# A transformer stack on one core: convolution inputs earlier in the mixing stage, output projection split 7 + 1, activation rows of 2048 bytes

## The chip, the cores and the metric

The kernel runs as one program on one core of a Trainium2 chip. The metric is device microseconds of one execution. All arithmetic is fp32; every dense product is built from three matmuls of a split number format (see below). TensorE (PE) does the matmuls, VectorE (DVE) and ScalarE (ACT) the elementwise work, GpSimd (POOL) a small triangular recurrence, and SyncE (SP) issues most of the DMA transfers.

## The reference, cut to what matters

Three residual blocks follow one another on a sequence of 512 tokens with 1024 channels: a token-mixing block with a first feed-forward network, then an attention block and a gated linear recurrence, each with a feed-forward network, on 528 tokens (16 meta tokens are put in front). The change concerns the first block, above all its token mixing:

```
p = h @ w_in
p_conv, p_rw = p[..., :2 * CONV_WIDTH], p[..., 2 * CONV_WIDTH:]
u, u_gate = jnp.split(p_conv, 2, axis=-1)
u = u * jax.nn.sigmoid(u_gate)
u = causal_dwconv(u, conv_dw_w, conv_dw_b)          # 31 taps, 512 channels
u = jax.nn.silu(layer_norm(u) * conv_ln_g + conv_ln_b)
...
y = wkv7_scan(rh, heads(decay), kh, vh, kk, heads(a))   # 8 heads of 64
...
m = jnp.concatenate([u, y], axis=-1) @ w_out            # 1024 x 1024
x = x + gt_m * rms_norm(m, mix_post_g)
h = rms_norm(x, ffn_pre_g) * (1.0 + sc_f) + sh_f        # input of the first FFN
f = channel_mix(h, w_up, ffn_dw_w, ffn_dw_b, w_down)    # 1024 -> 5632 -> 1024
```

## The kernel before, in words

Channels lie on the 128 partitions and tokens along the free dimension, so an activation of 1024 channels is eight K tiles of 128 x 512. A dense product splits its operands into a high and a low part: activations into xh and xl, weights into wh (a cast on ACT, L167) and wl (a subtraction on DVE, L168). For each K tile three matmuls follow: xh with wh, xh with wl, xl with wh (L192, L193, L194; all are called `mm` after the PSUM tile they write). The PSUM pool of `mm` has two buffers, and each is emptied by ACT or DVE before it is used again.

The two tiles xh and xl hold the input of whichever dense product comes next. Each has eight rows per partition, one per K tile, of 544 floats (2176 bytes), and 512-token stages read from an offset within a row (SEG1). The feed-forward's hidden activations, gh and gl, have rows of 512 floats (2048 bytes).

**The mixing stage** works on four pairs of heads. `wkv_prep` makes the operands of a pair; `wkv_inverse` inverts 128 x 128 triangles in blocks of doubling size (POOL does the smallest blocks, PE matmuls L714 to L751 the others); `wkv_tail` goes through four chunks of the sequence (L766 to L795) and then normalises: a per-token statistic by matmul (L274), a reciprocal square root of eleven small DVE operations on 128 x 8 (L294 to L305), a broadcast back by matmul (L285), the gate (L803, L804) and the product with it (L805). Beside it four convolution tiles are made: `conv_in(i)` is two dense products of 24 matmuls, `conv(i)` the first tap on ACT and 30 taps on DVE (L496, 120 in all). `ada_tile` multiplies 24 weight tiles with the conditioning vector on DVE (L328), as they arrive by DMA.

`mix_out` ends the stage: the output projection, in which the concatenated K tiles are three wkv tiles (pairs 0 to 2), four convolution tiles and the fourth wkv tile. The convolution tiles need the layer norm over all 512 channels (`conv_tail`, L541 to L564), the last wkv tile the tail of pair 3. Before, K tiles 0 to 2 are multiplied first for all eight output tiles (72 matmuls, parked by an ACT copy, L894), and the other five for the first four output tiles at 512 columns and for the last four in two token halves (`dense_ends`; DVE adds L905 and L909). Then RMS norm, residual (`post`, L814 and L815), second RMS norm (L849) and the FFN's input (L926 to L928), each per half.

The order of instructions on an engine is set by a scheduler with priorities: what is written in a `with filler(k)` block takes a very low priority, so it goes where an engine has nothing more urgent, and its place among the rest is not seen in the code.

## Time and profile before

| | |
|---|---|
| median of 3 runs | 2323.74 us (2323.18 to 2327.2) |
| profiled execution | 2322.99 us |
| its span, first to last instruction | 2319.9 us |
| mean granted TensorE clock | 0.987 |
| mixing stage | 0 to 471.6 us of the span |
| first FFN | 471.6 to about 850 us |

The profile gives each engine's busy time, the rows of each instruction with its start within the span, the idle time before it and what ended that idle time. Matmuls overlap in the array: a row's own duration includes the drain, so the price of a matmul in a stream is the distance from its start to the start of the next.

### The profile page before, as it was taken

The page shows a single profiled execution, that of the slowest core. Times are in us where ns is not written, and L with a number is a line of the kernel's source. Part 1 is how long each engine was busy: PE and PEld are TensorE (multiplying, and loading weights), DVE is VectorE, ACT ScalarE, POOL GpSimd, SP SyncE. Part 2 cuts the span into 40 slices and gives each one's busy share as a digit, 9 for nine tenths or more (in the row PEclk, how much of TensorE's full clock was granted, in tenths as well). Part 3 has the DMA queues.
Part 4 walks back from the last instruction along what each step waited for, and adds up shares of the span by engine and source line. Part 5 has one row for each costly group of instructions (what it writes and reads, how often), then busy time and mean ns, then how long its engine had stood idle before and what let it go on. Part 6 is the DMA issues. An engine that isn't in the chain of part 4 may idle for free.

```text
span 2319.9 us, 38166 instructions
## 1 busy us (share of the span) xinstructions
PE 2245.9 (97%) x15368; PEld 1986.3 (86%) x15368; DVE 1428.8 (62%) x3061; ACT 963.0 (42%) x1898; POOL 73.1 (3%) x163
## 2 busy tenths in 40 slices
PE   7989898899999999999999999999999999999999
PEld 4657675678888889988799999999999999999888
DVE  6856777775553376666676666435666667666522
ACT  3533234544442365566654444324333335444311
POOL 1140320000000000000000000000000000000000
PEclk8999999899999999999999999999999999999999
DMA  8443321252223432221032222333121113232232
GB/s 306 140 132 107 97 54 53 86 163 94 97 91 92 128 121 85 71 74 56 31 109 92 91 91 86 92 88 120 56 65 56 53 38 113 91 98 94 89 118 75
DMA packets 97487, 220.10 MB, mean 95 GB/s; under 512 B 21264, under 2 KB 43024, under 8 KB 97312
## 3 DMA queue, kind: packets, MB, share of 16 engines
q1 hardware_dynamic: 94112, 213.84, 29.3%
q10 hardware_dynamic: 2912, 3.69, 0.5%
q8 instruction: 121, 1.98, 0.4%
q0 software_dynamic: 288, 0.15, 0.1%
q14 instruction: 54, 0.44, 0.1%
HBM read 211.24 MB, written 6.85 MB: 94 GB/s over the span
## 4 chain that ended last, share of the span: by engine, by line
PE 85%; DVE 6%; DMA 3%; ACT 2%; POOL 2%; issue 1%; SPq 0%; ACTq 0%; DVEq 0%; POOLq 0%
PE mm L193 23%; PE mm L192 23%; PE mm L194 23%; PE sb L1385 3%; DVE wl L168 1%; PE sc L1200 1%; POOL Tb L698 1%; PE sb L1175 1%; DMA wa<-ada_wT 1%; PE sc L1218 1%; POOL tm L696 1%; ACT wh L167 1%; PE sa L849 1%; PE sa L1105 1%; PE sa L658 0%
## 5 line engine op out<-in xcount | busy, mean ns | idle before, releaser
L192 PE MATMUL mm<-xh,wh 128*128 128x264 f32 (+4 forms) x2852 | 906.2, 318 | 11.2 <-ACT xh L251 5.7
L193 PE MATMUL mm<-xh,wl 128*128 128x264 f32 (+4 forms) x2852 | 898.6, 315 | 2.3 <-DVE wl L168 2.1
L194 PE MATMUL mm<-xl,wh 128*128 128x264 f32 (+4 forms) x2852 | 896.5, 314 | 0.1
L192 PEld LDWEIGHTS mm<-xh,wh 128*128 128x128 f32 x2852 | 535.4, 188 | 48.4 <-ACT xh L251 6.7
L193 PEld LDWEIGHTS mm<-xh,wl 128*128 128x128 f32 x2852 | 537.0, 188 | 39.9 <-DVE wl L168 4.5
L168 DVE TENSOR_TENSOR wl<-ws,wh 128x1024 fp32r<-128x1024 f32 (+3 forms) x358 | 399.4, 1116 | 273.3 <-ACT wh L167 272.3
L194 PEld LDWEIGHTS mm<-xl,wh 128*128 128x128 f32 x2852 | 535.5, 188 | 34.4 <-issue 3.4
L167 ACT CAST wh<-ws 128x1024 fp32r<-128x1024 f32 (+3 forms) x358 | 344.7, 963 | 470.6 <-PE mm L194 402.4
L193 PE MATMUL mm<-gh,wl 128*128 128x264 f32 (+2 forms) x792 | 253.3, 320 | 1.3 <-DVE wl L168 0.9
L192 PE MATMUL mm<-gh,wh 128*128 128x264 f32 (+2 forms) x792 | 253.0, 319 | 0.0
L194 PE MATMUL mm<-gl,wh 128*128 128x264 f32 (+2 forms) x792 | 252.7, 319 | 0.0
L193 PEld LDWEIGHTS mm<-gh,wl 128*128 128x128 f32 x792 | 149.6, 189 | 13.3 <-DVE wl L168 2.8
L192 PEld LDWEIGHTS mm<-gh,wh 128*128 128x128 f32 x792 | 149.5, 189 | 10.4
L194 PEld LDWEIGHTS mm<-gl,wh 128*128 128x128 f32 x792 | 149.6, 189 | 10.3
L959 DVE SCALAR_TENSOR_TENSOR fz<-mm,V,fz 128x511 f32<-128x511 f32 x88 | 65.9, 748 | 69.7 <-ACT fz L957 68.1
L496 DVE SCALAR_TENSOR_TENSOR h<-u,cw,h 128x512 f32<-128x512 f32 x120 | 90.1, 753 | 3.7 <-ACT h L494 2.9
L1385 PE MATMUL sb<-q,kt 128*128 128x64 f32 (+3 forms) x592 | 75.4, 271 | 2.3 <-DVE kt L1417 2.3
L1385 PEld LDWEIGHTS sb<-q,kt 128*128 128x128 f32 x592 | 73.3, 195 | 2.8 <-DVE kt L1417 1.0
L193 PE MATMUL mm<-oh,wl 128*128 128x264 f32 x256 | 75.0, 293 | 0.5 <-DVE wl L168 0.5
L192 PE MATMUL mm<-oh,wh 128*128 128x264 f32 x256 | 74.6, 291 | 0.0
L194 PE MATMUL mm<-ol,wh 128*128 128x264 f32 x256 | 74.4, 291 | 0.0
L957 ACT ACTIVATE fz<-mm,V 128x512 f32<-128x512 f32 x44 | 34.3, 779 | 67.8 <-PE mm L194 67.7
(499 smaller groups left out, 2781.8 us busy)
## 6 DMA issues: line engine op xcount, KB each, us to landing
ws<-w_up_t SPq DMA_DIRECT2D x44, 512.0 KB, 3.7
ws<-gate_t SPq DMA_DIRECT2D x44, 512.0 KB, 3.7
ws<-up_t SPq DMA_DIRECT2D x44, 512.0 KB, 3.6
...
```

The costliest lines, as they stand in the source:

```text
L167: nc.scalar.copy(hi[:, :n], st[:, :n])
L168: nc.vector.tensor_sub(lo[:, :n], st[:, :n], hi[:, :n])
L192: mm(o, hi[:, w], xh[i][:, a:b], start=start and i == 0, stop=False)
L193: mm(o, lo[:, w], xh[i][:, a:b], start=False, stop=False)
L194: mm(o, hi[:, w], xl[i][:, a:b], start=False, stop=stop and i == n - 1)
L496: nc.vector.scalar_tensor_tensor(acc, src, w, acc, MULT, ADD)
L696: nc.gpsimd.tensor_tensor(tm[:, 0:n, 0:w], Gb[:, j, w:].unsqueeze(2).to_broadcast([64, n, w]), Tb[:, j, 0:w].unsqueeze(1).to_broadcast([64 ...
L698: nc.gpsimd.tensor_tensor(o, o, tm[:, 0:n, 0:w], op=ADD)
L849: nc.tensor.matmul(sq.ps[:, :n], k.mean, t, start=i == 0, stop=i == KD - 1)
L957: nc.scalar.activation(z, ps, AF.Identity, bias=vec("ffn_dw_b", nt), scale=wt(2))
L959: nc.vector.scalar_tensor_tensor(z[:, t:], ps[:, 0:T1 - t], wt(2 - t), z[:, t:], MULT, ADD)
L1385: nc.tensor.matmul(o, kt[:, a:a + P], qv, start=True, stop=True)
```

## The change

Three things change, and all of them keep the arithmetic.

First, the rows: within the 512-token stages (mixing and the first FFN) xh and xl are now read through views x1h and x1l, whose rows have 512 floats (2048 bytes). For the later stages the rows become 530 floats (2120 bytes). The two columns of zeros at the head of the later rows are written after the first FFN.

Second, the convolution: `conv_in(1)`, `conv_in(2)` and `conv_in(3)` stand ahead of the tails of pairs 0, 1 and 2, and all taps are fillers.

Third, the output projection: K tiles 0 to 6 of all output tiles first, then K tile 7 for the eight output tiles, all at 512 columns; the squares for the RMS norm are summed by matmul (L853 in the changed kernel, L849 before) instead of by DVE adds, and there is one reciprocal square root over 512 columns where there were two over 256.

```diff
-SEG1 = [(2, 514)]
-SEG1X = [(2, 258), (258, 514)]
+SEG1 = [(0, T1)]
+SEG1X = [(0, H1), (H1, T1)]
...
-    k.xh, k.xl = (k.res.tile([P, KD, T2 + 16], F32R, name=n)[:, :, 6:6 + T2 + 2] for n in ("xh", "xl"))
-    nc.gpsimd.memset(k.xh[:, :, 0:2].bitcast(F32), 0.0)
-    nc.gpsimd.memset(k.xl[:, :, 0:2].bitcast(F32), 0.0)
+    both = [k.res.tile([P, 67 * 64], F32R, name=n) for n in ("xh", "xl")]
+    k.xh, k.xl = (t[:, :KD * (T2 + 2)].rearrange("p (k t) -> p k t", k=KD) for t in both)
+    k.x1h, k.x1l = (t[:, :KD * T1].rearrange("p (k t) -> p k t", k=KD) for t in both)
...
+        def conv_late(i):
+            with filler(k):
+                conv(i)
+
         conv_in(0)
         gates()
-        conv(0)
+        conv_late(0)
         wkv_inverse(k, Q[0])
+        conv_in(1)
         wkv_tail(k, Q[0])
         Q[2] = pair(2)
+        conv_late(1)
         wkv_inverse(k, Q[1])
-        conv_in(1)
+        conv_in(2)
         wkv_tail(k, Q[1])
-        conv(1)
+        conv_late(2)
         Q[3] = pair(3)
-        conv_in(2)
         wkv_inverse(k, Q[2])
-        with filler(k):
-            conv(2)
+        conv_in(3)
+        conv_late(3)
         wkv_tail(k, Q[2])
-        conv_in(3)
         wkv_inverse(k, Q[3])
-        conv(3)
...
+        conv_tail(k, p2, S.acc_u)
         for i in range(KD):
-            if i == 2:
-                conv_tail(k, p2, S.acc_u)
-            dense(k, A["w_out_t"][i], k.xh, k.xl, SEG1, lambda j, ps: nc.scalar.copy(m[i], ps), kts=(3,))
+            dense(k, A["w_out_t"][i], k.x1h, k.x1l, SEG1, lambda j, ps: nc.scalar.copy(m[i], ps), kts=(7,))
...
-    def evac(i, j, ps):
-        if j is None:
-            nc.vector.tensor_add(m[i], m[i], ps)
-            add_square(k, sq, i, 0, m[i], T1)
-            return
-        mt = m[i][:, hs(j)]
-        nc.vector.tensor_add(mt, mt, ps[:, 0:H1])
-        add_square(k, sq, i, H1 * j, mt, H1)
-        if i == KD - 1:
-            rms_scale(k, sq, H1 * j, H1, r[j])
+    def evac(i, ps):
+        nc.vector.tensor_add(m[i], m[i], ps)
+        add_square(k, sq, i, 0, m[i], T1, True)
+
+    for i in range(KD):
+        dense(k, A["w_out_t"][i][:, 7 * P:], k.x1h, k.x1l, SEG1, lambda _, ps: evac(i, ps), kts=(1,), x0=7)
     r = p2.tile([P, T1], F32, name="r", tag="tl", bufs=1)
+    rms_scale(k, sq, 0, T1, r, True)
     r = [r[:, hs(j)] for j in range(2)]
-    w = [A["w_out_t"][i][:, 3 * P:] for i in range(KD)]
-    dense_ends(k, w, k.xh, k.xl, SEG1X, evac, 4, SEG1[0], kts=(5,), x0=3)
...
-        nc.gpsimd.memset(k.rp[:, 0:2], 0.0)
+        for t in (k.rp[:, 0:2], *(t[:, :, 0:2].bitcast(F32) for t in (k.xh, k.xl))):
+            nc.gpsimd.memset(t, 0.0)
```

How the engines' orders move is shown at three places. The line numbers are each kernel's own; in this part of the changed kernel they are one to four higher than before.

PE at the end of the inverse of pair 0 and the start of its tail, before (X, Dt and NM are operands of the recurrence, `mm` the dense products):

```order
L742 MATMUL sb<-Dt,ys 64x64 x4
L751 MATMUL sb<-X,Dt 128x128 x8
L766 MATMUL sa<-NM_106,X 64x128 x2
L771 MATMUL sa<-tok,X 128x128
L766 MATMUL sa<-NM_106,X 64x128 x2
L771 MATMUL sa<-tok,X 128x128
L766 MATMUL sa<-NM_106,X 64x128 x2
```

The same place in the changed kernel, the last seven rows from where the dense run ends:

```order
L755 MATMUL sb<-X,Dt 128x128 x8
L194 MATMUL mm<-xh,wl 128x512
L195 MATMUL mm<-xl,wh 128x512
L193 MATMUL mm<-xh,wh 128x512
...
L193 MATMUL mm<-xh,wh 128x512
L194 MATMUL mm<-xh,wl 128x512
L195 MATMUL mm<-xl,wh 128x512
L770 MATMUL sa<-NM_104,X 64x128 x6
L775 MATMUL sa<-tok,X 128x128 x2
L782 MATMUL sa<-tok 128x128
L783 MATMUL sa<-X,tok 128x128
```

Between the last matmul of the inverse and the first of the tail now stand 26 dense matmuls of 512 columns; before there was none. Between the statistic (L274, now L275) and the broadcast (L285, now L286) of that tail there are 45 of them, before 12.

DVE in the tail of pair 3, from the statistic onward, before (rsxb, tstb and rstb are the small operands of the reciprocal square root, `h<-u,cw,h` is a tap of the convolution, wl a split of weights):

```order
L305 TENSOR_SCALAR rsxb<-sb 128x8
L496 SCALAR_TENSOR_TENSOR h<-u,cw,h 128x512
L294 TENSOR_SCALAR tstb<-rsxb 128x8
L168 TENSOR_TENSOR wl<-ws,wh 128x384
L496 SCALAR_TENSOR_TENSOR h<-u,cw,h 128x512
L295 TENSOR_SCALAR tstb<-tstb 128x8
L496 SCALAR_TENSOR_TENSOR h<-u,cw,h 128x512
L297 TENSOR_TENSOR rstb<-tstb 128x8
L168 TENSOR_TENSOR wl<-ws,wh 128x384
L496 SCALAR_TENSOR_TENSOR h<-u,cw,h 128x512
L298 SCALAR_TENSOR_TENSOR rstb<-rstb,rsxb 128x8
```

The same in the changed kernel:

```order
L306 TENSOR_SCALAR rsxb<-sb 128x8
L295 TENSOR_SCALAR tstb<-rsxb 128x8
L296 TENSOR_SCALAR tstb<-tstb 128x8
L298 TENSOR_TENSOR rstb<-tstb 128x8
L299 SCALAR_TENSOR_TENSOR rstb<-rstb,rsxb 128x8
L300 SCALAR_TENSOR_TENSOR tstb<-rstb,tstb 128x8
L298 TENSOR_TENSOR rstb<-tstb 128x8
```

No tap and no split of weights stands between the small operations any more; all taps lie ahead of this tail. On PE, no dense matmul stands in the tail of pair 3 either, where 54 stood before.

PE at the end of the output projection in the changed kernel, with buffer numbers (mm_3319 is the seven-K-tile part of the last output tile, mm_3447, mm_3462 and mm_3476 the one-K-tile parts of the first three, sa_3460 the sum of squares):

```order
L193 MATMUL mm_3319<-xh_88,wh_3322 128x512
L193 MATMUL mm_3447<-xh_88,wh_3450 128x512
L194 MATMUL mm_3447<-xh_88,wl_3451 128x512
L195 MATMUL mm_3447<-xl_89,wh_3450 128x512
L194 MATMUL mm_3319<-xh_88,wl_3323 128x512
L195 MATMUL mm_3319<-xl_89,wh_3322 128x512
L193 MATMUL mm_3319<-xh_88,wh_3322 128x512
L194 MATMUL mm_3319<-xh_88,wl_3323 128x512
L193 MATMUL mm_3462<-xh_88,wh_3465 128x512
L194 MATMUL mm_3462<-xh_88,wl_3466 128x512
L195 MATMUL mm_3462<-xl_89,wh_3465 128x512
L853 MATMUL sa_3460<-nsq_3458,mean_79 128x512
```

It goes on so, three matmuls and one square at a time, to the eighth one-K-tile part, and only then come the last 13 matmuls of mm_3319. Before, the same engine ran through four groups of 15 matmuls at 512 columns and eight of 15 at 256:

```order
L192 MATMUL mm_3431<-xh_88,wh_3434 128x512
L193 MATMUL mm_3431<-xh_88,wl_3435 128x512
L194 MATMUL mm_3431<-xl_89,wh_3434 128x512
L192 MATMUL mm_3457<-xh_88,wh_3460 128x256
L193 MATMUL mm_3457<-xh_88,wl_3461 128x256
L194 MATMUL mm_3457<-xl_89,wh_3460 128x256
```

## Rows read from the trace of the kernel before

**Rows 1.** The page: busy time, share of the span and instructions of each engine.

```profile
PE 2245.9 (97%) x15368; PEld 1986.3 (86%) x15368; DVE 1428.8 (62%) x3061; ACT 963.0 (42%) x1898; POOL 73.1 (3%) x163
```

**Rows 2.** Stretches: us, busy us (count) of PE, PEld, DVE, ACT, POOL, PEclk, DMA.

```profile
368.60:405.30 36.70, 29.68 (x149) 19.49 (x148) 28.55 (x58) 16.54 (x28) 0.10 (x1) 0.97 0.22 67
405.30:437.20 31.90, 31.66 (x182) 27.77 (x182) 20.90 (x38) 17.93 (x30) 0.00 (x0) 0.92 0.39 116
437.20:460.00 22.80, 12.34 (x39) 8.74 (x40) 22.51 (x57) 12.57 (x32) 0.00 (x0) 0.78 0.04 11
...
471.60:784.00 312.40, 311.37 (x1337) 251.65 (x1338) 171.09 (x213) 122.53 (x159) 0.00 (x0) 1.00 0.35 108
```

**Rows 3.** Timeline of PE, first FFN, up projection (start us, us, what).

```profile
559.71 0.40 PE L192 MATMUL mm<-xh,wh 128*128 128x512 f32 x1
...
561.82 0.39 PE L192 MATMUL mm<-xh,wh 128*128 128x512 f32 x1
```

**Rows 4.** Timeline of PE, first FFN, down projection.

```profile
769.82 0.39 PE L194 MATMUL mm<-gl,wh 128*128 128x512 f32 x1
...
771.86 0.39 PE L194 MATMUL mm<-gl,wh 128*128 128x512 f32 x1
```

**Rows 5.** Groups of PE by shape, 471.6 to 784.3 us (busy us, mean ns).

```profile
L193 PE MATMUL mm<-xh,wl 128*128 128x512 f32 x336 | 133.6, 398 | 1.0 <-DVE wl L168 1.0
```

**Rows 6.** Groups of PE by shape, 784 us to the end.

```profile
L192 PE MATMUL mm<-xh,wh 128*128 128x264 f32 x1368 | 400.9, 293 | 1.5 <-DVE z L1012 1.0 <-DVE q L1340 0.5
...
L192 PE MATMUL mm<-xh,wh 128*128 128x258 f32 x344 | 97.4, 283 | 0.0
...
L192 PE MATMUL mm<-xh,wh 128*128 128x512 f32 x168 | 66.6, 397 | 0.0
```

**Rows 7.** Timeline of PE in the last FFN, 258 columns.

```profile
2059.98 0.28 PE L192 MATMUL mm<-xh,wh 128*128 128x258 f32 x1
...
2061.78 0.28 PE L192 MATMUL mm<-xh,wh 128*128 128x258 f32 x1
```

**Rows 8.** Timeline of PE, tail of pair 0.

```profile
167.71 0.44 PE L766 MATMUL sa<-NM,X 128*64 128x128 f32 x4
...
174.55 0.79 PE L778 MATMUL sa<-tok 128*128 128x128 f32 x2 [2.78 <-DVE ar L767]
...
188.46 0.95 PE L274 MATMUL sa<-cf,sq 128*128 128x2 f32 x8
...
194.88 1.09 PE L285 MATMUL sa<-cf,tsta 128*64 128x128 f32 x16
```

**Rows 9.** Timeline of DVE, reciprocal square root in the tail of pair 3.

```profile
384.25 0.17 DVE L305 TENSOR_SCALAR rsxb<-sb 128x8 f32<-128x8 f32 x1 [0.17 <-PE sb L274]
...
390.19 0.17 DVE L298 SCALAR_TENSOR_TENSOR rstb<-rstb,rsxb 128x8 f32<-128x8 f32 x1
390.39 0.17 DVE L299 SCALAR_TENSOR_TENSOR tstb<-rstb,tstb 128x8 f32<-128x8 f32 x1
...
392.91 0.16 DVE L299 SCALAR_TENSOR_TENSOR tstb<-rstb,tstb 128x8 f32<-128x8 f32 x1
...
396.90 0.69 DVE L805 TENSOR_TENSOR h<-y,sb 128x512 f32<-128x512 f32 x1 [0.56 <-PE sb L804]
```

**Rows 10.** Timeline of PE, tail of pair 3.

```profile
368.59 0.44 PE L766 MATMUL sb<-NM,X 128*64 128x128 f32 x4
...
405.31 0.80 PE L192 MATMUL mm<-xh,wh 128*128 128x512 f32 x1 [5.68 <-ACT xh L251]
```

**Rows 11.** Timeline of PE, last matmul of the output projection.

```profile
436.69 0.28 PE L194 MATMUL mm<-xl,wh 128*128 128x256 f32 x1
```

**Rows 12.** Timeline of DVE, first norm to FFN input.

```profile
441.56 0.42 DVE L564 SCALAR_TENSOR_TENSOR r<-rsq 128x256 f32<-128x256 f32 x1
...
457.65 2.35 DVE L168 TENSOR_TENSOR wl<-ws,wh 128x1024 fp32r<-128x1024 f32 x2
...
467.67 0.89 DVE L928 SCALAR_TENSOR_TENSOR xl<-hn,mod,xh 128x256 fp32r<-128x256 f32 x2 [0.18 <-ACT xh L927]
```

More of the change, by code (lines that the diff above doesn't have):

```diff
@@ L393, in start @@
         nc.vector.scalar_tensor_tensor(x[:, i], x[:, i], ga[:, i:i + 1], rs, MULT, MULT)
-        hi, sh = k.xh[:, i, 2:2 + T1], k.mod[:, i:i + 1]
+        hi, sh = k.x1h[:, i], k.mod[:, i:i + 1]
         nc.scalar.activation(hi, x[:, i], AF.Identity, bias=sh)
-        nc.vector.scalar_tensor_tensor(k.xl[:, i, 2:2 + T1], x[:, i], sh, hi, ADD, SUB)
+        nc.vector.scalar_tensor_tensor(k.x1l[:, i], x[:, i], sh, hi, ADD, SUB)
         w = slice(i * P, (i + 1) * P)
         for (h, l), o in zip(W, O):
-            xh, xl = k.xh[:, i, 2:2 + T1], k.xl[:, i, 2:2 + T1]
+            xh, xl = k.x1h[:, i], k.x1l[:, i]
             mm(o, h[:, w], xh, start=i == 0, stop=False)
@@ L458, in win @@
         def win(nt, evac):
-            dense(k, A["w_in_t"][nt], k.xh, k.xl, SEG1, evac)
+            dense(k, A["w_in_t"][nt], k.x1h, k.x1l, SEG1, evac)
         S.gd = p1.tile([P, T1], F32, name="gd")
@@ L465, in gates @@
             win(21, lambda j, ps: shift_mix(k, ps, S.gd, 13))
-            dense(k, A["w_in_e"], k.xh, k.xl, SEG1, lambda j, ps: shift_mix(k, ps, S.gd1, 14, 32), m=32)
+            dense(k, A["w_in_e"], k.x1h, k.x1l, SEG1, lambda j, ps: shift_mix(k, ps, S.gd1, 14, 32), m=32)
             sigmoid(k, S.gd, S.gd)
@@ L553, in conv_tail @@
         nc.scalar.activation(o, acc_u[:, i], AF.Silu, bias=vec("conv_ln_b", i), scale=vec("conv_ln_g", i))
-        split(k, k.xh[:, 3 + i, 2:2 + T1], k.xl[:, 3 + i, 2:2 + T1], o)
+        split(k, k.x1h[:, 3 + i], k.x1l[:, 3 + i], o)
 def newton(k, s, y2, out, eps, neg, y=None):
@@ L886, in mix_out @@
     hs = lambda j: slice(H1 * j, H1 * j + H1)
-    xt = lambda i: (k.xh[:, i, 2:2 + T1], k.xl[:, i, 2:2 + T1])
+    xt = lambda i: (k.x1h[:, i], k.x1l[:, i])
     with filler(k):
@@ L924, in mix_out @@
             t = p2.tile([P, T1], F32, name="hn", tag="tmp")[:, :H1]
-            sh, hi = k.mod[:, 24 + i:25 + i], k.xh[:, i, a:b]
+            sh, hi = k.mod[:, 24 + i:25 + i], k.x1h[:, i, a:b]
             nc.vector.scalar_tensor_tensor(t, x[:, i], k.gn[:, i:i + 1], rn[:, hs(j)], MULT, MULT)
             nc.scalar.activation(hi, t, AF.Identity, bias=sh)
-            nc.vector.scalar_tensor_tensor(k.xl[:, i, a:b], t, sh, hi, ADD, SUB)
+            nc.vector.scalar_tensor_tensor(k.x1l[:, i, a:b], t, sh, hi, ADD, SUB)
 def conv3(k, src, w, b, out, n):
@@ L961, in up @@
             if w is None:
-                dense(k, A["w_up_t"][nt], k.xh, k.xl, SEG1, evac)
+                dense(k, A["w_up_t"][nt], k.x1h, k.x1l, SEG1, evac)
             return evac
@@ L977, in ffn_first @@
         w = A["w_up_t"]
-        dense_start1(k, [w[0], w[KF]], k.xh, k.xl, [up(KF * t, f, w) for t, f in enumerate(pair(0))])
+        dense_start1(k, [w[0], w[KF]], k.x1h, k.x1l, [up(KF * t, f, w) for t, f in enumerate(pair(0))])
         for i in range(1, KF):
```

## The prediction

> **What bounds the kernel now.** I read the page first: PE is busy for 97% of the span, DVE for 62% [rows 1]. Then the table of stretches, since that share is a mean over unlike stages. In the first FFN PE is busy in 311.4 of 312.4 us [rows 2]: there only the price of a matmul counts. In the tail of pair 3 PE is busy for 29.7 of 36.7 us and DVE for 28.6, and after the output projection PE for 12.3 of 22.8 us at a granted clock of 0.78 while DVE is busy nearly throughout [rows 2]: there a chain of small steps sets the time, and a matmul moved out of it, or a tap on DVE, is worth what it delays the chain. So two sums are wanted, one of matmul prices for the FFN, one walk along the chain for mixing.
>
> **The rows.** The price of a streamed matmul is the distance of starts. In the up projection (xh, rows of 2176 bytes) nine steps take 561.82 - 559.71 = 2.11 us, 234.4 ns each [rows 3]. In the down projection (gh, rows of 2048 bytes) nine steps take 771.86 - 769.82 = 2.04 us, 226.7 ns each [rows 4]. Both have 512 columns, the clock is 1.00 throughout [rows 2], the weights lie in the same tiles. What differs is where the moving operand lies: from the program's memory plan, the xh rows start 32 bytes past a multiple of 256 from the weights and shift by 128 with every row, the gh rows start on a multiple. The x1h and x1l rows will start as the gh rows do. The up projection has 3 x 336 = 1008 matmuls [rows 5]; 1008 x 7.7 ns = **7.8 us less**. The bounds: nothing, if the stride is not the cause, and 7.8. I take 7.8, because no other difference between the two streams is left to see.
>
> A rule speaks against it. The Trainium skill ("TensorE: Matmul & The Clock Gate", section "Step-by-step: what each phase is for") says that PE reads the moving operand and the weights through two independent ports, so that loading weights takes no bandwidth from a running matmul. By it the placement of one against the other would be worth 0 instead of 7.8 us. The trace does not test this, as no stream of before changes its rows alone.
>
> The later stages get rows of 2120 bytes, which no row of before has. Their matmuls of 264 and 258 columns and the 504 of 512 come to 3 x 1368 + 3 x 344 + 3 x 168 = 5640 in the shapes shown [rows 6]. At 258 columns the price is now (2061.78 - 2059.98) / 15 = 120.0 ns [rows 7], that is 12.5 ns over 258 columns at 2.4 GHz; gh at 512 has 13.4 over its 213.3, xh 21.1. So the short ones already pay no more than the well placed stream. I take 0. The bounds: a gain of 504 x 7.7 ns = 3.9 us, if the long ones are cured too, and a loss of 7.7 ns on the other 5136, 39.5 us. The zero columns, now written by POOL after the first FFN, cost nothing: POOL is busy for 73 us in all [rows 1].
>
> **Convolution inputs and taps.** The PE order puts 26 dense matmuls ahead of the tail of pair 0: 26 x 0.227 = 5.9 us, so its first matmul goes from 167.71 to about 173.6. But this tail loses 2.78 us at 174.55 to a DVE step [rows 8], which now has that time to end in, and it holds 14 fewer dense matmuls up to the statistic (20 for 34, 14 x 0.234 = 3.3 us). So the statistic stays near 188.5 [rows 8]. From there to the broadcast stand 45 dense matmuls in place of 12: 45 x 0.227 = 10.2 us and one or two of small steps against 6.4 us now [rows 8], so the broadcast comes near 200, some **5 us late**, and pair 2 with it, since its preparation is queued behind on PE. Later the debt is paid back in part: from the broadcast of tail 1 to the start of tail 3 stand 46 dense matmuls where there were 65, 19 x 0.23 = 4.4 us less. Up to the start of tail 3 both orders hold the same number of dense matmuls. Walking along, I get +2.8 us at the start of tail 3, less 0.8 for some hundred matmuls on the path that are 7.7 ns cheaper: **+2 us**. Bounds: 0, as PE does the same work, and +6, if nothing of the debt comes back.
>
> In tail 3 DVE's small chain takes from 384.25 to 393.07 [rows 9], 8.8 us for eleven steps, because every step stands behind a tap or a split of weights; two undisturbed steps are 0.20 us apart [rows 9], eleven are 2.3 us. Less **6.5 us**. No dense matmul is left in this tail (28 stood ahead of the statistic): about 2 us less on its path. The convolution's layer norm came behind the product with the gate, 8.4 us from 396.90 to 405.31 [rows 9, 10]. Its statistics now stand ahead of it; three scalings on DVE at 0.69 us, as that product [rows 9], and two ACT steps about as long are left, some 4 us: 4.4 less. Together 13 us, so the four convolution tiles are there at 405.3 + 2 - 13 = **394.3** instead of 405.31 [rows 10].
>
> **Output projection.** Here the change gives back what it won. Before, 72 matmuls lay under tail 3, and from 405.31 to the last matmul at 436.69 [rows 11] only five K tiles were left. Now 18 lie ahead of the tail, and by the order 133 follow before the first one-K-tile group: 133 x 0.227 = 30.2 us, to 424.5. Then the last seven-K-tile part holds one of the two `mm` buffers, unfinished, so the eight groups of three matmuls all go through the other: three starts and a drain (2 x 0.227 + 0.39 [rows 4]), a DVE add of 512 columns (0.69 [rows 9]) and about 0.12 of hand-over make 1.66 us a group; seven of them and the last one's 0.7 make 12.3 us where the matmuls alone need 5.4. Then 13 x 0.227 = 3.0 us of matmuls, to 440. From the last matmul to the first norm's result took 441.98 - 436.97 = 5.0 us [rows 11, 12] at 256 columns. At 512 I count seven steps (copy, add, square, reciprocal root and its square, two of Newton) at 0.69, the sum's matmul at 0.39 and some 0.6 of hand-overs: 5.8 us. So the result is there at **445.7, +3.7 us**.
>
> What follows is DVE's: from 441.56 to 467.67 + 0.89 [rows 12] 27 us. Nine residual steps that were done ahead of it now follow (9 x 0.42, the row of 256 columns, = 3.8 us); the two weight splits (2.35 us [rows 12]) go ahead. **+1.4 us.** Mixing thus ends 5.1 us later than now; its bounds are +16 (the tail's 13 us halved, the debt of 6 kept) and -4 (no debt, groups at matmul rate).
>
> **The sum.** -7.8 + 5.1 = -2.7 us. The profiled execution took 2322.99 us (span 2319.9, 3.1 around it); it lies 0.75 below the median of the three runs. Against the median: 2323.74 - 2.7 = **2321.0**, 0.12% less. Within 0.2% (4.6 us), about what a measurement of this kernel tells from no change. This case, 45%, has a range of its own of 2316 to 2326.
>
> **Rivals.**
> - *The groups do not queue, 22%.* If the one-K-tile groups follow one another at matmul rate (other work of DVE out of the way, the second buffer free early), 6.9 us fall away: 2314.1. For it: DVE has only these adds to do there. Against: the order leaves one buffer open.
> - *The rows change nothing, 13%.* Without the 7.8 us: 2328.8, at the edge of slower. For it: no stream of before changes its rows alone. Against it: the two streams have no other difference. The Trainium skill's rule named above would have it so.
> - *The clock falls at the end of the projection, 12%.* The queue of groups keeps PE about half busy, as in the stretch after 437.2 us, whose clock is 0.78 [rows 2]. At 1.2 GHz three starts and the drain take 0.6 us more a group, 4.8, and the last 13 matmuls 0.2 each, 2.6: +7.4, 2328.4.
> - *Rows of 2120 bytes are worse, 8%: slower.* The 5136 short matmuls of the later stages are the place; 1.4 ns on each, 7.3 us, decides for slower. At half of what the bad rows cost now, 3.9 ns, it is +20: 2341. For it: 2120 is no multiple of 32. Against: the short ones pay nothing for 2176.
>
> **How the numbers follow.** Faster by over 0.2% (below 2319.1): a third of the forecast's case and nearly all of the first rival, 0.37. Slower (above 2328.4): half of the second and third rival and most of the last, 0.19. Same: 0.44. The range, 2311 to 2331, leaves out the lower edge of the first rival and the last rival.
>
> **What would show it.** The distance of starts in the up projection: 227 right, 234 wrong. In the later stages 120 at 258 columns. The first matmul of tail 0 near 173.6, its broadcast near 200; tail 3 starting near 370.6; its small chain 2 to 3 us long; dense matmuls on convolution tiles from 394; the groups 1.66 us apart on PE; the FFN's gapless stretch starting near 476. It is wrong if the debt of pair 2 is kept to the end, if the groups overlap, or if any stream after 850 us has another price.

## The result and the profile after

| | before | after |
|---|---|---|
| median | 2323.46 us (2322.72 to 2327.2, 4 runs) | 2357.83 us (2349.28 to 2360.76, 4 runs) |
| ratio after to before | | 1.0133, interval 1.0105 to 1.0161 |
| profiled execution, its span | 2322.99, 2319.9 us | 2349.28, 2347.3 us |

The change is slower: by 1.3% in the ratio, which is 31 us, and by 34 us in the medians. The forecast of 2321.0 and its range to 2331 both fail. The execution profiled after the change is the fastest of its four, 8.5 us below their median, so the trace shows less of the loss than the medians do.

The page of after, busy time by engine, answers to [rows 1]:

```profile
PE 2261.0 (96%) x15320; PEld 1999.9 (85%) x15320; DVE 1421.6 (61%) x3040; ACT 960.6 (41%) x1888; POOL 74.7 (3%) x163
```

PE holds 15.1 us more busy time with 48 instructions fewer, and outside its busy time the span has grown by another 12.3. So two things went wrong at once: some matmuls became dearer, and PE stands idle more. The table of stretches says where (us, busy us and count of PE, PEld, DVE, ACT, POOL, granted clock, DMA share, GB/s). Its rows are the tail of pair 3, the projection on the convolution tiles, the norms behind it, and the up projection, as in [rows 2]:

```profile
385.60:407.80 22.20, 17.71 (x95) 9.45 (x94) 13.07 (x33) 9.62 (x15) 0.10 (x1) 0.88 0.00 1
407.80:458.60 50.80, 50.08 (x188) 35.82 (x188) 18.10 (x29) 20.66 (x35) 0.00 (x0) 0.95 0.23 70
458.60:481.40 22.80, 10.99 (x34) 8.52 (x34) 17.46 (x42) 11.33 (x22) 0.00 (x0) 0.69 0.12 44
503.40:816.00 312.60, 312.13 (x1392) 259.31 (x1393) 172.42 (x214) 123.16 (x162) 0.23 (x2) 0.99 0.35 111
```

The tail of pair 3 became short as forecast (22.2 for 36.7 us), but it starts 17 us later, and the stretch behind it took 50.8 us where 31.7 were needed. The clock after the projection is 0.69, before it was 0.78. Over the mixing stage the stretches granted only 1.2 GHz add up to 105.8 us, before to 54.6 (the last of them reaches 4.7 us into the FFN).

The first FFN did what was forecast. PE's timeline in the up projection, against [rows 3]:

```profile
559.65 0.39 PE L195 MATMUL mm<-xl,wh 128*128 128x512 f32 x1
...
561.46 0.39 PE L194 MATMUL mm<-xh,wl 128*128 128x512 f32 x1
```

Eight steps in 1.81 us, 226 ns each, where [rows 3] gave 234.4.

PE's timeline in the tail of pair 0, which answers to [rows 8]: first matmul of the tail, statistic, broadcast.

```profile
182.24 0.88 PE L770 MATMUL sa<-NM,X 128*64 128x128 f32 x12
...
193.82 0.61 PE L275 MATMUL sa<-cf,sq 128*128 128x2 f32 x4
...
205.18 0.66 PE L286 MATMUL sa<-cf,tsta 128*64 128x128 f32 x8
```

The first matmul, forecast near 173.6, is at 182.24, the statistic, forecast near 188.5, at 193.82, and the broadcast is 10.3 us late (194.88 before), twice the forecast. The clock was at 1.2 GHz from 163.3 to 177.0. PE's timeline from the statistic of tail 2 to the first matmul of the inverse of pair 3, then the first matmul of tail 3 and the first on a convolution tile, against [rows 10]; the bracket is idle time and what ended it:

```profile
341.85 1.05 PE L275 MATMUL sa<-cf,sq 128*128 128x2 f32 x8 [0.75 <-ACT sq L802]
356.15 0.79 PE L718 MATMUL sb<-Dm,NM 128*128 128x128 f32 x2 [13.24 <-DMA Dm<-Dd]
...
385.55 0.44 PE L770 MATMUL sb<-NM,X 128*64 128x128 f32 x4
...
407.83 0.80 PE L193 MATMUL mm<-xh,wh 128*128 128x512 f32 x1 [1.95 <-ACT xh L252]
```

This is the largest hole of the new kernel. PE waits 13.24 us for the blocks that POOL hands over by DMA. In the kernel before, the same wait was 2.40 us:

```profile
343.31 1.16 PE L714 MATMUL sb<-Dm,NM 128*128 128x128 f32 x8 [2.40 <-DMA Dm<-Dd]
```

The blocks come late because POOL is late. Its last small block of pair 3, before:

```profile
336.72 0.63 POOL L700 COPY Tt<-Tb 64x256 f32<-64x256 f32 x1
```

and after:

```profile
349.50 1.11 POOL L704 COPY Tt<-Tb 64x256 f32<-64x256 f32 x1
```

Before, POOL was done 0.9 us ahead of the statistic of tail 2 (338.21), after, 8.8 us behind it (341.85). That is 9.6 of the 10.8 us by which the hole grew. Another 1.6 us are the seven dense matmuls that stood between that statistic and the inverse, where none stands now; the way from POOL's last block to PE became 0.4 us shorter. DVE's chain in tail 3, against [rows 9]:

```profile
398.45 0.17 DVE L306 TENSOR_SCALAR rsxb<-sb 128x8 f32<-128x8 f32 x1 [1.81 <-PE sb L275]
...
400.67 0.17 DVE L300 SCALAR_TENSOR_TENSOR tstb<-rstb,tstb 128x8 f32<-128x8 f32 x1
```

It lasts 2.4 us, forecast 2.3, before 8.8. DVE's timeline in the projection and the norms, against [rows 11, 12]: L907 are the adds of the one-K-tile groups, L169 the splits of weights, L567 and L568 the first norm, L924 and L926 the FFN's input.

```profile
442.15 0.69 DVE L907 TENSOR_TENSOR ar<-ar,mm 128x512 f32<-128x512 f32 x1 [1.21 <-PE mm L195]
...
453.03 0.69 DVE L907 TENSOR_TENSOR X<-X,mm 128x512 f32<-128x512 f32 x1 [0.92 <-PE mm L195]
...
459.75 1.23 DVE L169 TENSOR_TENSOR wl<-ws,wh 128x1024 fp32r<-128x1024 f32 x1 [2.60 <-ACT wh L168]
460.89 0.68 DVE L907 TENSOR_TENSOR y<-y,mm 128x512 f32<-128x512 f32 x1
464.92 0.69 DVE L567 SCALAR_TENSOR_TENSOR rsq<-sa,rsq 128x512 f32<-128x512 f32 x1 [3.35 <-ACT rsq L566]
465.65 0.69 DVE L568 SCALAR_TENSOR_TENSOR r<-rsq 128x512 f32<-128x512 f32 x1
...
477.07 1.27 DVE L924 SCALAR_TENSOR_TENSOR hn<-h,gn,rn 128x256 f32<-128x256 f32 x3
...
497.20 0.89 DVE L926 SCALAR_TENSOR_TENSOR xl<-hn,mod,xh 128x256 fp32r<-128x256 f32 x2 [0.18 <-ACT xh L925]
```

The groups are (453.03 - 442.15) / 6 = 1.81 us apart. The norm's result is there at 466.34, before at 441.98, and the last input of the FFN at 498.1, before at 468.6.

### The profile page after: what moved, and what is told of

Same layout as the page of the kernel before. It is cut to its first block, busy times and chain, and to the rows that moved or that the text cites. A ratio compares the mean times of both kernels' runs of the same rounds, so it can differ in the third digit from the quotient of the medians.

```text
span 2347.3 us, 38037 instructions
## 1 busy us (share of the span) xinstructions
PE 2261.0 (96%) x15320; PEld 1999.9 (85%) x15320; DVE 1421.6 (61%) x3040; ACT 960.6 (41%) x1888; POOL 74.7 (3%) x163
## 4 chain that ended last, share of the span: by engine, by line
PE 88%; DVE 5%; ACT 2%; DMA 2%; POOL 1%; issue 1%; SPq 0%; ACTq 0%; DVEq 0%; POOLq 0%
PE mm L193 24%; PE mm L194 24%; PE mm L195 23%; PE sb L1384 3%; DVE wl L169 1%; PE sc L1199 1%; PE sb L1174 1%; PE sa L853 1%; PE sc L1217 1%; PE sa L662 1%; POOL tm L700 1%; ACT wh L168 1%; POOL Tb L702 1%; PE sa L1104 1%; DMA wa<-ada_wT 1%
## 5 line engine op out<-in xcount | busy, mean ns | idle before, releaser
L193 PE MATMUL mm<-xh,wh 128*128 128x264 f32 (+5 forms) x2832 | 904.9, 320 | 12.2 <-ACT xh L925 5.7
L194 PE MATMUL mm<-xh,wl 128*128 128x264 f32 (+5 forms) x2832 | 894.1, 316 | 2.2 <-DVE wl L169 2.0
L195 PE MATMUL mm<-xl,wh 128*128 128x264 f32 (+5 forms) x2832 | 890.8, 315 | 0.7 <-DVE xl L253 0.6
L193 PEld LDWEIGHTS mm<-xh,wh 128*128 128x128 f32 (+1 forms) x2832 | 534.4, 189 | 55.0 <-ACT wh L168 8.3
L169 DVE TENSOR_TENSOR wl<-ws,wh 128x1024 fp32r<-128x1024 f32 (+4 forms) x354 | 396.4, 1120 | 292.1 <-ACT wh L168 291.4
L194 PEld LDWEIGHTS mm<-xh,wl 128*128 128x128 f32 (+1 forms) x2832 | 534.7, 189 | 35.7 <-DVE wl L169 4.5
L195 PEld LDWEIGHTS mm<-xl,wh 128*128 128x128 f32 (+1 forms) x2832 | 534.8, 189 | 33.6 <-issue 2.1
L168 ACT CAST wh<-ws 128x1024 fp32r<-128x1024 f32 (+4 forms) x354 | 341.9, 966 | 472.0 <-PE mm L195 404.9
L957 DVE SCALAR_TENSOR_TENSOR fz<-mm,V,fz 128x511 f32<-128x511 f32 (+1 forms) x88 | 65.7, 749 | 68.6 <-ACT fz L955 67.1
```

The source lines that it names most:

```text
L168: nc.scalar.copy(hi[:, :n], st[:, :n])
L169: nc.vector.tensor_sub(lo[:, :n], st[:, :n], hi[:, :n])
L193: mm(o, hi[:, w], xh[i][:, a:b], start=start and i == 0, stop=False)
L194: mm(o, lo[:, w], xh[i][:, a:b], start=False, stop=False)
L195: mm(o, hi[:, w], xl[i][:, a:b], start=False, stop=stop and i == n - 1)
L957: nc.vector.scalar_tensor_tensor(z[:, t:], ps[:, 0:T1 - t], wt(2 - t), z[:, t:], MULT, ADD)
```

## The experiments

The theory: both edits of the mixing stage cost time, the rows gain. The convolution inputs, moved forward, lengthen the path and leave PE nothing to do while pair 3 waits for POOL. The projection exposes matmuls that lay under tail 3, then queues. The rivals: rows of 2120 bytes take the FFN's gain back in the later stages; the loss is the lowered clock alone; the groups queue for a PSUM buffer alone.

The first four kernels take the parts of the change one at a time; the other seven each undo, fill or move one suspected cost. Prices are taken from ratios times 2325 us (medians of the kernel before in the three sets of runs were 2325.83, 2324.09 and 2326.86), and places from the traces. The two are kept apart, since one profiled execution may lie off its median: those of E3, E4 and E7 lie 6 to 8 us below it, that of E5 7 us above. The three sets ran on three chips, each beside the kernel before.

| kernel | median us | ratio to before | interval |
|---|---|---|---|
| E1 rows alone | 2319.93 | 0.9977 | 0.9961 to 0.9994 |
| E2 rows, projection | 2350.46 | 1.0100 | 1.0078 to 1.0122 |
| E3 rows, conv inputs, taps | 2339.5 | 1.0053 | 1.0030 to 1.0076 |
| E4 rows, taps | 2320.57 | 0.9975 | 0.9962 to 0.9988 |
| E5 E2, own PSUM buffers | 2348.65 | 1.0098 | 1.0072 to 1.0124 |
| E6 E3, conv_in(3) back | 2329.37 | 1.0023 | 1.0007 to 1.0039 |
| E7 E3, hole filled | 2343.21 | 1.0068 | 1.0041 to 1.0095 |
| E8 E4, late rows 2176 | 2316.97 | 0.9969 | 0.9952 to 0.9986 |
| E9 E2, groups last | 2347.62 | 1.0078 | 1.0052 to 1.0104 |
| E10 E1, no halves | 2326.25 | 0.9994 | 0.9982 to 1.0007 |
| E11 E4, conv_in(1) forward | 2325.12 | 0.9987 | 0.9973 to 1.0001 |

Moments of the traces, us of the span: the ACT cast of the first convolution tile (which answers to 405.31 in [rows 10], less its own time), the end of the last projection matmul, the first FFN input of each half, the 88th DVE step on fz (the up projection's outputs), the end, and the sum of the stretches at 1.2 GHz in the mixing stage.

```
         cast   last mm  half 0  half 1  up proj.  end     1.2 GHz
before   404.7  437.0    448.8   461.9   711.3     2319.9   54.6
after    407.2  458.6    477.1   491.4   735.8     2347.3  105.8
E1       405.8  437.9    449.9   463.1   705.0     2317.3   61.4
E2       408.7  460.0    478.4   491.8   737.9     2349.8   99.0
E3       408.2  449.9    461.8   475.3   717.4     2330.0   92.2
E4       401.9  433.5    445.1   458.2   700.1     2312.7   68.3
E5       413.8  464.6    483.0   496.4   741.2     2354.0  109.2
E6       403.2  444.8    457.6   471.1   713.1     2325.7   81.9
E7       410.1  452.3    465.1   478.7   720.6     2333.3   88.7
E8       407.0  438.9    450.7   463.8   705.7     2315.0   75.1
E9       408.3  458.2    476.1   490.5   735.0     2346.4   92.2
E10      404.3  434.6    453.4   467.8   712.2     2323.7   75.1
E11      412.3  443.8    455.4   468.5   710.4     2322.9   81.9
```

### E1: the rows alone

The mixing stage's order and the projection are those of before; only the rows are the new ones.

```diff
-SEG1 = [(2, 514)]
+SEG1 = [(0, T1)]
...
-    dense_ends(k, w, k.xh, k.xl, SEG1X, evac, 4, SEG1[0], kts=(5,), x0=3)
+    dense_ends(k, w, k.x1h, k.x1l, SEG1X, evac, 4, SEG1[0], kts=(5,), x0=3)
```

> The kernel before with the new rows alone (2048 bytes up to the first FFN, 2120 after). Both theories: starts in the up projection 227 ns apart, 258 columns still 120 ns, mixing ends where it did (471 us of the span), 7.8 us less in the first FFN: 2315.5 us.

Measured: 0.9977, 5.3 us less. PE's timeline in the up projection of E1:

```profile
552.93 0.39 PE L193 MATMUL mm<-xh,wh 128*128 128x512 f32 x1
...
555.20 0.39 PE L194 MATMUL mm<-xh,wl 128*128 128x512 f32 x1
```

Ten steps in 2.27 us: 227 ns. With nothing else changed, the place of the moving rows is worth 7 to 8 ns on a matmul of 512 columns, and the rival that it is worth nothing falls. Some is given back: from the step on fz to the end E1 takes 1612.3 us, before 1608.6.

### E2: rows and projection

E1 with the whole third part of the change (K tiles 7 + 1, squares by matmul, one norm); the convolution is as before.

```diff
-            dense(k, A["w_out_t"][i], k.x1h, k.x1l, SEG1, lambda j, ps: nc.scalar.copy(m[i], ps), kts=(3,))
+            dense(k, A["w_out_t"][i], k.x1h, k.x1l, SEG1, lambda j, ps: nc.scalar.copy(m[i], ps), kts=(7,))
```

> New rows and the 7 + 1 projection, convolution inputs and taps where they were before. Theory P (the projection lost its cover: from the first matmul on convolution tiles to the FFN's gapless stream it took 66 us before and 100 in the change): that stretch again near 95 to 100 us, half clock in it, 2340 us or more. Theory C (the convolution inputs moved forward take the cover from later waits, the clock falls there, and what follows only inherits it): the stretch near 75 us, 2318 to 2325 us.

Measured: 1.0100, that is 28.6 us more than E1, as theory P has it. By the moments, E2 less E1: 2.9 us at the cast, 19.2 from there to the last matmul, 6.4 to half 0, 0.2 to half 1, 4.2 to the step on fz; -0.4 after it. The 19.2 can be worked out: behind the cast stand 174 matmuls, at 0.227 us 39.5 us; E1 has 60 at 512 columns and 120 at 256 (0.120 each), 28.0; so 11.5 are exposed work. Seven group distances of 1.81 in place of 0.68 are another 7.9; E9 shows what most of them are.

### E3: rows, convolution inputs and taps

E1 with the whole second part of the change; the projection is 3 + 5 as before.

```diff
         wkv_inverse(k, Q[0])
+        conv_in(1)
         wkv_tail(k, Q[0])
...
-        conv_in(1)
+        conv_in(2)
         wkv_tail(k, Q[1])
...
+        conv_in(3)
+        conv_late(3)
         wkv_tail(k, Q[2])
-        conv_in(3)
         wkv_inverse(k, Q[3])
```

> New rows and the convolution moved as in the change (inputs forward, all taps fillers), projection 3 + 5 as before. Theory P: start of pair 3's tail at most 8 us late, its tail some 10 us shorter, the rest 66 us: 2308 to 2315 us. Theory C: half clock near 130 to 146, 163 to 177 and 344 to 365 us as in the change, pair 3's tail starts some 15 us late and the total is 2322 us or more.

Measured: 1.0053, 17.7 us more than E1, as theory C has it. PE's timeline of E3 at the start of the inverse of pair 3:

```profile
352.09 2.08 PE L718 MATMUL sb<-Dm,NM 128*128 128x128 f32 x8 [14.20 <-DMA Dm<-Dd]
```

The hole is there without the new projection. From 340 to 360 us E3 has no record of a dense matmul, E4, next, has 22; but E4 has no hole to fill there, as its POOL is done 4.2 us before the statistic of tail 2 (335.2 and 339.4 us), that of E3 9.2 us behind it (346.0 and 336.8).

### E4: rows and taps

E1 with every `conv(i)` in its old place, as a filler.

```diff
-        conv(0)
+        conv_late(0)
...
-        conv(1)
+        conv_late(1)
...
-        conv(3)
+        conv_late(3)
```

> New rows, all taps as fillers, but the convolution inputs and the projection where they were before. If the early inputs do the harm (theory C): half clock in mixing as in the kernel before (some 55 us), 2312 to 2319 us. If the taps' low priority does it: pair 3's tail or the layer norm waits for taps, more half clock, 2322 us or more. Theory P has no opinion beyond 2316 us.

Measured: 0.9975, the same as E1 within the intervals. Taps as fillers cost nothing that these runs can tell; the 18.1 us between E4 and E3 belong to the convolution inputs alone. The stretches at 1.2 GHz before 177 us do not: E4 has them as well (126.6 to 143.6 and 160.7 to 174.4 us), E1 much less (135.0 to 145.2 and 175.9 to 179.3). POOL too is slower in the kernels with the moved inputs. The table of stretches while POOL does the small blocks of pair 3, of E4:

```profile
321.20:335.20 14.00, 14.00 (x117) 10.27 (x114) 7.67 (x15) 4.90 (x13) 11.66 (x31) 1.00 0.05 15
```

and of after:

```profile
331.90:350.60 18.70, 10.26 (x61) 7.29 (x59) 16.73 (x36) 0.96 (x2) 16.36 (x31) 0.83 0.08 26
```

The same 31 POOL instructions take 14.0 us with DVE busy for 7.7, and 18.7 with DVE busy for 16.7 (E3: 17.65 with 13.9; before: 14.3 with 9.7). Two of them of one shape, from POOL's timeline of after:

```profile
331.89 0.21 POOL L700 TENSOR_TENSOR tm<-Gb,Tb 64x15 f32<-64x15 f32 x1 [54.31 <-DMA Gb<-Ld]
...
347.97 0.68 POOL L700 TENSOR_TENSOR tm<-Gb,Tb 64x15 f32<-64x15 f32 x1
```

The same shape takes three times as long at 348 us, where DVE runs one tap after another. Of POOL's 30 small products in after, 15 start while a tap runs and take 0.59 to 0.80 us; 14 of the others take 0.21 to 0.32. In E4 8 start beside a tap. The Trainium skill ("SBUF — State Buffer", section "Who interferes with whom") says that a DVE instruction with two SBUF inputs, as a tap is, contends with a GpSimd instruction that reads SBUF. The traces agree, by 0.21 against 0.68 us. No run took the taps away from POOL's time and left all else, so its share of the total, some 4 us by the lengths above, is a reading, not a test.

### E5: the groups in PSUM buffers of their own

E2 with the one-K-tile groups in three buffers of another PSUM pool.

```diff
-        dense(k, A["w_out_t"][i][:, 7 * P:], k.x1h, k.x1l, SEG1, lambda _, ps: evac(i, ps), kts=(1,), x0=7)
+        hl = wload(k, A["w_out_t"][i][:, 7 * P:], 1)
+        ps = bank(k, "b")
+        products(k, hl, ps, [k.x1h[:, 7]], [k.x1l[:, 7]], 0, T1, True, True)
+        evac(i, ps)
```

> As e2_rows_proj, but the eight one-K-tile groups write into the three buffers of the pool that the inverse used, not into the one mm buffer left. If the groups' queue is a main part of what the 7 + 1 split costs (they took 14 us in the change, 1.81 us each, where their matmuls need 5.4): groups 1 us apart or less, 6 to 9 us less than e2_rows_proj, 2341 to 2345 us. If the loss is the cover that the 72 early matmuls gave (PE idle and at half clock in and before pair 3's tail, everything after it exposed): within 3 us of e2_rows_proj's 2350.

Measured: 1.0098, no different from E2; the groups are 1.72 us apart for 1.81. So the PSUM buffer alone is not what holds them. The weights' pool has two buffers too, and the unfinished part holds one of them: by the trace the next group's ACT cast waits for PE to finish the group before, the split on DVE for the cast and for the add, and PE for both. The rival of a PSUM queue alone falls.

### E6: conv_in(3) back behind tail 2

```diff
-        conv_in(3)
-        conv_late(3)
         wkv_tail(k, Q[2])
+        conv_in(3)
+        conv_late(3)
         wkv_inverse(k, Q[3])
```

> As e3_rows_conv, but conv_in(3) stands behind the tail of pair 2 again. Theory C1 (the 48 matmuls of conv_in(3) covered PE's wait for POOL and the transfers of pair 3's inverse; without them PE idles 14 us and runs at half clock for 20): the idle time before the first large matmul of that inverse under 5 us, no half clock at 338 to 359 us, 2322 to 2328 us. Theory C2 (conv_in(1) ahead of tail 0 delays pair 2 and all that follows): 2333 us or more.

Measured, in E3 otherwise: 1.0023, 7.0 us less than E3 (the intervals overlap at their ends), between the ranges of the two theories. PE's timeline of E6 at the same place:

```profile
352.25 2.07 PE L718 MATMUL sb<-Dm,NM 128*128 128x128 f32 x8 [11.03 <-DMA Dm<-Dd]
```

The hole is only 3 us smaller, so theory C1 fails in its first sign: POOL is done as late as in E3 (345.8 and 346.0 us). Of the 48 matmuls put back, 10 run between the statistic of tail 2 and the hole, 21 behind it (35 dense records from 350 to 400 us, E3 has 14). The gain is behind the hole: from this row to tail 3 it takes 26.2 us, in E3 31.5, with 6.3 us of it at 1.2 GHz for 17.2, so that tail 3 starts at 378.5 for 383.6.

### E7: the hole filled with matmuls of no use

E3 with 48 matmuls behind tail 2, of which eight columns go into a spare tile that nothing reads.

```diff
+        def idle():
+            for _ in range(2):
+                ps = k.psd.tile([P, 512], F32, name="mm")
+                for n in range(24):
+                    nc.tensor.matmul(ps, k.x1h[:, n % 8, 0:P], k.x1h[:, n % 8], start=n == 0, stop=n == 23)
+                nc.scalar.copy(spare[:, 0:8], ps[:, 0:8])
...
         wkv_tail(k, Q[2])
+        idle()
         wkv_inverse(k, Q[3])
```

> As e3_rows_conv, with 48 added matmuls of 512 columns behind the tail of pair 2 whose result is not used: the cover of conv_in(3) without its content. If the granted clock is what the missing cover costs there: full clock in 338 to 359 us, the inverse of pair 3 from its first large matmul to the tail in 25 to 27 us instead of 31.5, 5 to 8 us less than e3_rows_conv, 2331 to 2335 us. If only the late start counts: 2339 us or more.

Measured: 1.0068, not below E3. PE's timeline of E7, the first of the added matmuls and the end of the hole:

```profile
334.98 0.48 PE L487 MATMUL mm<-xh 128*128 128x512 f32 x1
...
358.70 2.08 PE L727 MATMUL sb<-Dm,NM 128*128 128x128 f32 x8 [6.48 <-DMA Dm<-Dd]
```

The hole is halved, and from here to tail 3 it takes 24.7 us where E3 took 31.5, with 3.9 us of it at 1.2 GHz for 17.2. But POOL's blocks are done at 353.0 for 346.0, so the walk starts 6.6 us later, and in the trace nothing is won at tail 3 (383.4 for 383.6). The added matmuls did not make it late: the first of them runs at 334.98, when tail 2 has already started, at 333.3 for 326.0 in E3. This execution was at 1.2 GHz from 229.5 to 236.4 and from 308.0 to 314.9 us, where that of E3 was not. So the traces price the low clock behind the hole, at 5 to 7 us in E6 and E7; whether buying it back with matmuls of no use would pay stays open, as the two ratios do not differ.

### E8: later rows of 2176 bytes again

E4 with 544 floats a row for the later stages, starting 14 floats in; the first stages stay at 2048 bytes.

```diff
-    both = [k.res.tile([P, 67 * 64], F32R, name=n) for n in ("xh", "xl")]
-    k.xh, k.xl = (t[:, :KD * (T2 + 2)].rearrange("p (k t) -> p k t", k=KD) for t in both)
-    k.x1h, k.x1l = (t[:, :KD * T1].rearrange("p (k t) -> p k t", k=KD) for t in both)
+    both = [k.res.tile([P, KD, T2 + 16], F32R, name=n) for n in ("xh", "xl")]
+    k.xh, k.xl = (t[:, :, 14:16 + T2] for t in both)
+    k.x1h, k.x1l = (t.rearrange("p k t -> p (k t)")[:, :KD * T1].rearrange("p (k t) -> p k t", k=KD) for t in both)
```

> As e4_rows_taps, but the stages after the first FFN have rows of 2176 bytes again (2048 up to there). The 264- and 266-column matmuls went up by 0.4 and 1.1 ns with 2120 bytes, 2.6 us in all. If that is the rows: 122 ns at 264 columns again, 2318 us, 2 to 3 us less than e4_rows_taps. If not: 2320 to 2321 us.

Measured: 0.9969, the fastest of all. Against E4 the difference of the ratios is inside the intervals, but the traces have it: from the step on fz to the end the two kernels with late rows of 2176 bytes take 1608.6 (before) and 1609.3 us (E8), the eleven with 2120 bytes 1611.4 to 1612.8. Distances of starts between neighbours of one shape at full clock, from the traces, mean ns over the count (distances above 0.2 us, at 512 columns 0.3, left out, as a record can be missing between two):

```
                before       E1           E4           E8
264 columns     121.83 3740  122.27 3731  122.26 3719  121.14 3731
266 columns     122.37 1008  123.53 1008  123.52 1008  123.57 1008
258 columns     119.50 1008  119.86 1008  119.86 1008  120.87 1008
512 columns     233.52  483  233.04  483  233.04  483  231.99  483
up proj. 512    234.44  977  226.71  981  226.67  962  226.72  981
```

So the prediction's slow rival is real and small: 0.4 to 1.2 ns on a short matmul from before to E4, some 3 us, not 20. What E8 takes back lies almost wholly in the 264 columns; the 266 did not come back, and the 258 became dearer. As its late rows start 14 floats in and those of before 6, length and start are not separated here either.

### E9: the groups behind the last seven-K-tile part

E2 with the groups as fillers too, so that no part is left unfinished while they run.

```diff
-    for i in range(KD):
-        dense(k, A["w_out_t"][i][:, 7 * P:], k.x1h, k.x1l, SEG1, lambda _, ps: evac(i, ps), kts=(1,), x0=7)
+    with filler(k):
+        for i in range(KD):
+            dense(k, A["w_out_t"][i][:, 7 * P:], k.x1h, k.x1l, SEG1, lambda _, ps: evac(i, ps), kts=(1,), x0=7)
```

> As e2_rows_proj, but the eight one-K-tile groups are fillers too, so that they follow the last seven-K-tile part instead of standing inside it. The unfinished part held one of two mm buffers and, as e5_proj_banks showed, one of the two weight buffers, so that each group's weights had to wait for the group before. Theory Q: with both weight buffers free the groups come about 1.1 us apart and the last matmul 6 to 8 us after the last seven-K-tile one instead of 17.8: 7 to 9 us less than e2_rows_proj, 2341 to 2344 us. If the adds and squares set the pace anyway: 2347 us or more.

Measured: 1.0078, 5.1 us less than E2, the intervals overlapping. DVE's timeline of E9, first add and seventh:

```profile
446.85 0.69 DVE L908 TENSOR_TENSOR ar<-ar,mm 128x512 f32<-128x512 f32 x1 [4.33 <-PE mm L195]
...
456.49 0.69 DVE L908 TENSOR_TENSOR X<-X,mm 128x512 f32<-128x512 f32 x1 [0.66 <-PE mm L195]
```

Still 1.61 us apart, though no unfinished part holds buffers any more. PE's timeline of E9, the last two matmuls of a group and the first record of the next, shows why; L854 is the sum of squares:

```profile
454.27 0.40 PE L194 MATMUL mm<-xh,wl 128*128 128x512 f32 x1
454.51 0.40 PE L195 MATMUL mm<-xl,wh 128*128 128x512 f32 x1
454.74 1.02 PE L854 MATMUL sa<-nsq,mean 128*128 128x512 f32 x2
455.20 0.79 PE L193 MATMUL mm<-xh,wh 128*128 128x512 f32 x1
```

Each sum of squares is two records on PE whose starts are 0.43 us apart (at 454.74 and 455.17), 0.86 us a group. With three matmuls of 0.227 that is 1.54 of the 1.61 us: here PE itself is full. The squares are there because the change took their sum from DVE's adds to a matmul; eight of them are 6.9 us of PE. So the groups could not come 1.1 us apart, and the second forecast of E9 (2347 us or more) is the one that held. No run kept the split and left the squares on DVE, so this part of the price is read from the trace, not tested.

### E10: the projection without halves

E1 with the five late K tiles at 512 columns for all eight output tiles, and one norm.

```diff
-    dense_ends(k, w, k.x1h, k.x1l, SEG1X, evac, 4, SEG1[0], kts=(5,), x0=3)
+    for i in range(KD):
+        dense(k, w[i], k.x1h, k.x1l, SEG1, lambda _, ps: evac(i, None, ps), kts=(5,), x0=3)
+    rfull = p2.tile([P, T1], F32, name="rfull", tag="tl", bufs=1)
+    rms_scale(k, sq, 0, T1, rfull)
```

> As e1_rows (split 3 + 5, the 72 early matmuls stay), but the five late K tiles of all eight output tiles at 512 columns, and one norm over 512 columns instead of two over 256. Theory H: the halves let the first norm and the residual of one half run beside the other half's matmuls; without them the way from the last matmul to the first FFN input takes 18 us instead of 11.7: 2325 to 2329 us. If the halves hide nothing that counts: 2318 to 2322 us, as e1_rows.

Measured: 0.9994, 4.0 us more than E1, in the range of theory H, though the intervals overlap. PE's timeline of E10, last projection matmul:

```profile
434.16 0.39 PE L195 MATMUL mm<-xl,wh 128*128 128x512 f32 x1
```

DVE's timeline of E10, the first input of the FFN:

```profile
453.39 1.27 DVE L933 SCALAR_TENSOR_TENSOR hn<-h,gn,rn 128x256 f32<-128x256 f32 x3
```

From the end of the last matmul to the first input 18.8 us pass, in E1 12.0, and half 0 of after has 18.4: as much is lost behind the last matmul where the halves alone are missing as in the whole change. With halves, the first half's norm and residual run while PE does the second half.

### E11: conv_in(1) forward alone

E4 with one convolution input moved.

```diff
         wkv_inverse(k, Q[0])
+        conv_in(1)
         wkv_tail(k, Q[0])
...
         wkv_inverse(k, Q[1])
-        conv_in(1)
         wkv_tail(k, Q[1])
```

> As e4_rows_taps, but conv_in(1) stands ahead of the tail of pair 0, as in the change (conv_in(2) and conv_in(3) where they were before). Theory C2: pair 2 starts 4 to 6 us later and the delay lasts: 2326 to 2331 us. Theory C1: the delay is absorbed where PE waits for pair 3's inverse, because conv_in(2) and conv_in(3) still cover it: 2319 to 2324 us.

Measured: 0.9987, 2.8 us more than E4, the intervals overlapping: by the median between the ranges of the two theories, by the ratio (2322.0) in that of C1. E4, E11, E6 and E3 are a ladder, one input more moved forward at each rung: +2.8, +8.4, +7.0 us. Only the middle rung is outside its intervals; the sum, 18.1, is far outside. E11's trace has the broadcast of tail 0 at 206.0, as late as after, and the wait at pair 3 still short (2.8 us): the hole comes with the second input moved. What changes there is the order on PE. In before and E11 the inverse of pair 2 starts behind the statistic in the preparation of pair 3 (291.8 behind 284.0 us; 292.6 behind 290.5); in after, E3 and E6, where `conv_in(2)` no longer stands between, it starts ahead of it (282.1 and 291.0; 279.7 and 285.6; 282.9 and 288.7). The last products of that preparation feed POOL, and POOL then starts after tail 2 (1.4, 2.4 and 5.0 us), not before it (3.0 and 4.5 us).

## Why the prediction was wrong, point by point

The miss against the profiled execution's span is 2347.3 - 2317.2 = 30.1 us: 26.7 at the start of the FFN (503.4, forecast 476.7), 2.9 in the later stages, 0.5 between.

**The rows, right in the FFN.** 226 to 227 ns as forecast, E1. The Trainium skill's rule on two independent ports, which the prediction weighed ("TensorE: Matmul & The Clock Gate", "Step-by-step: what each phase is for"), does not make placement worth nothing: only the rows changed in E1, and the price fell from 234.4 to 227. Which of start and stride does it was not separated. The term "I take 0" for the later stages was off by 2.9 us; E8 takes most of that back.

**The step that failed first: "+2 us" at the start of tail 3.** It was +17.0 (385.6 for 368.6). The prediction walked along PE: it counted matmuls between events at full price and let the debt of tail 0 be paid back. The count was right, 522 dense records up to tail 3 in both traces, and on PE the debt did come back, from 15.1 us at the start of tail 1 to 4.4 at that of tail 2 (PE's wait for a transfer of weights at 278.5 us, 9.65 us long before, is 3.04 after). What it left out is the other path. Pair 3's inverse does not wait for PE but for POOL and the DMA behind it, and there 504 dense records, not 480, now stand ahead of tail 2, and the inverse of pair 2 ahead of the preparation that feeds POOL. Along this path the traces of before and after give the 17.0: POOL starts 8.9 us later (331.89 for 323.04), takes 4.4 longer beside the bunched taps, its results reach PE 0.4 sooner, and the inverse takes 4.1 more (29.4 for 25.3), 15.4 us of it at 1.2 GHz. E3 against E4, where the inputs alone differ (and E4's PE does not wait there at all), gives 7.2, 3.6, -0.7 and 6.3, together 16.5. Shown by runs: E3, E4, E6 and E11 put 18 us on the convolution inputs, E11 and E6 most of it on the second and third. Read from the traces: how it divides.

**Tail 3, right.** 22.2 us where 36.7 - 13 = 23.7 was forecast, small chain 2.4 us. But a tail 14.5 us shorter is no gain of 14.5: work that lay under it has to go elsewhere.

**The projection, mis-sized.** It was to go from 394.3 to 440, 45.7 us; it took 50.8, from 407.83 to 458.63. The groups did queue (1.81 us, forecast 1.66), but not for the PSUM buffer alone: without it 1.72 (E5), and without the weights' queue too 1.61 (E9), as the sum of squares holds PE for 0.86 us a group, which the sum left out along with four matmuls among the first groups (0.9 us). That the forecast came so near is partly luck. And the start of the stretch, 402.3 to 412.5, ran at 1.2 GHz, which the sum had at full clock. The first norm took 7.7 us from the last matmul, forecast 5.8, as a cast and a split of 1024 weight columns (1.23 us) got ahead of the last copy and add, and as the last sum of squares took 1.12 us for 0.39. "+1.4" behind it was +5.1 up to the last input (31.7 us for 26.6), and the FFN's gapless start came 2.3 us later behind that than before. The missing halves were priced at 0.8 us in the norm and 1.4 behind it; E10 puts 4.0 us on them in the total and 6.8 in its trace up to the first input.

**The sum, and what stays open.** By the ratios: rows -5.3, taps -0.5, convolution inputs +18.1, projection +28.6 (E2), together +40.9; measured +30.9. Beside the moved inputs, the projection costs only 18.6 (after against E3). Both edits use up the same cover, the dense work under tail 3: E3 too has more matmul records behind the cast than E4 (207 for 182), so part of that loss is counted twice. The traces put nearly all of it there: from the cast to the last projection matmul E1 takes 32.1 us, E3 41.7, E2 51.3 and after, with both, 51.4. No run tests it apart.

**The rivals.** That the groups do not queue: no. That the rows change nothing: no. That the clock falls: yes, far beyond the place named; by the traces it cost 5 to 7 us behind the hole of pair 3 (E6, E7). That rows of 2120 bytes decide: real, but some 3 us for 20. A case in which both moves lose was in none of the four, and the range's upper bound, "tail halved, debt of 6 kept", was the nearest.

E8 is faster than both kernels (0.9969): the new rows where they help, the old row length later, taps as fillers, and neither of the two moves.
